# Experts with 96 slots a round in place of 128, in a two-layer decoder trunk

## The chip, the cores and the metric

The kernel runs on one core of one Trainium2 chip. The metric is the time of the execution on the device in microseconds (us), as the median of several runs; lower is better. The core's engines work side by side, each on its own list of instructions in order: TensorE (PE: matmuls, with its weight loads shown apart as PEld), VectorE (DVE), ScalarE (ACT), GpSimd (POOL) and SyncE (SP), whose queue issues nearly all DMA transfers.

## The reference

A trunk of two layers over 256 tokens of width 1024, in float32. Layer 0 is an RWKV-7 mixing followed by a dense SwiGLU, layer 1 a dilated attention followed by a mixture of 8 experts. The change touches the experts alone. In short:

```python
logits = ht @ router                        # 256 tokens x 8 experts
top_logit, top_idx = lax.top_k(logits, 2)   # two experts for each token
top_w = softmax(top_logit)
# for every expert e, over the tokens xe that chose it:
gt, up = split(xe @ w_gu[e])                # 1024 -> 2 x 3584
y = (silu(gt) * up) @ w_down[e]             # 3584 -> 1024
out[token] += y * weight of e for the token
```

The result goes through `x <- LayerNorm(sqrt(2)*x + (1+gate)*out)` and is the output. How many tokens choose an expert depends on the data; 256 is the most. The mean is 64.

## The kernel before

**The order of the work.** Up to the experts, an order written by a planner in the Python code holds: its class `Engine` (line 125) estimates what each instruction costs and when its inputs are due, and every task yields what it waits for. The routing task (`route_task`, line 2079) belongs to that part; it makes the first expert's slots and its dispatch. From `run_experts` (line 2184) on, instructions go to their engines in the order of the code, and a framework sets semaphores for each data dependency. Its scheduler may move an instruction that depends on little, such as the transfer of line 2244, ahead within its queue. Nearly every instruction is recorded through the helper on line 191, so the profile shows that line for most, and groups are told apart by the names of tiles.

**What an expert does.** Each token has, for each expert that it chose, a rank among that expert's tokens (`rank`, with large negative numbers for the others). `slots` compares the rank with the row `iota` 0, 1, 2, ... and gets a 0/1 matrix `P` of 2 x 128 tokens by 128 slots. `disp` multiplies the hidden states `hn` by `P`: the columns of `xh` and `xl` are the tokens in their slots, split into a float32r part and the rest. `slots_t` makes the transpose `PT` for the way back.

The weights come in pieces of 1 MB (`wstream`), and `split` makes `whi` (ScalarE) and `wlo` (VectorE) of each. `mm3` issues three matmuls for each weight tile: `xh*whi`, `xh*wlo`, `xl*whi`. The token operand (128 rows x 128 slots) is the stationary one, which a weight load brings into the array; 512 weight columns move. `gate` and `up` run over 8 tiles of 128 rows each for one of 7 stretches of 512 hidden columns; the product `e_s` is transposed by `tr` (four 128 x 128 transposes on TensorE, where `e_s` is stationary and the identity moves), split into `ah` (ScalarE) and `al` (VectorE), and `down` multiplies it by 4 tiles of 128 x 1024, accumulating in two PSUM banks. `fin` splits the sum into `yh` and `yl`, and `back` multiplies by `PT` and adds the weighted result to `macc`.

`run_experts` weaves these together: `tr` of the stretch before is issued inside `gate`, `down` of the stretch before comes between `gate` and `up`, and the slots and dispatch of the next expert (`part`) are issued inside `up` of stretch 4.

**What is left over.** An expert with more than 128 tokens has ranks of 128 and above, which match no slot. For these the code writes a table with ranks reduced by 128 to DRAM (lines 2237 to 2244), loads the highest count into a register (line 2245) and has an `If` around a loop over all 8 experts (line 2246):

```python
cv = nc.values_load(cmaxi[0:1, 0:1], min_val=0, max_val=512)
with tc.If(cv > 128):
    with tc.For_i(0, NE, 1) as ei:
```

After it comes the last LayerNorm, which begins with `bn_stats` on VectorE.

Of the kernel before, what the change touches and what calls it, by code (L numbers as in the profile page):

```python
# [24 lines left out]
F32 = mybir.dt.float32  # L25
F32R = mybir.dt.float32r
# [3 lines left out]
OP = mybir.AluOpType  # L30
AX = mybir.AxisListType

D = 1024
S = 256
DFF = 2816
NE = 8
# [5 lines left out]
RANK0 = 1000  # L42
NEG = -1.0e30
CW = 1029


def _consts():
# [44 lines left out]
def tile_kernel(ctx: ExitStack, tc: tile.TileContext, cst_d, att_d, x, c, ada_w, ada_b, ln_g, ln_b, mu, w_rkv,  # L92
# [3 lines left out]
    SY = nc.sync  # L96
# [97 lines left out]
    V, SC, GP, PE = Engine(nc.vector, "V"), Engine(nc.scalar, "SC"), Engine(nc.gpsimd, "GP"), Engine(nc.tensor, "PE")  # L194
# [9 lines left out]
    adap = ctx.enter_context(tc.tile_pool(name="adap", bufs=1, reuse_waits="tile"))  # L204
    kq = ctx.enter_context(tc.tile_pool(name="kq", bufs=1, reuse_waits="tile"))

    def mmt(j=None, shape=(128, 512)):
        if j is None:
            j = mm_n[0] = (mm_n[0] + 1) % 4
        return ringed(("mm", j), 1, mm_pool.tile(list(shape), F32, name="mmb", tag=f"mmb{j}"))  # L210
# [59 lines left out]
    ident, triS, iota = (cst[:, i:i + 128] for i in (0, 128, 256))  # L270
# [15 lines left out]
    ps = pst((128, 120))  # L286
# [7 lines left out]
    ps = pst((128, 112))  # L294
# [153 lines left out]
    def mm3(ps, lh, ll, rh, rl, start, stop):  # L448
        PE.matmul(ps, lh, rh, start=start, stop=False)
        PE.matmul(ps, lh, rl, start=False, stop=False)  # L450
        PE.matmul(ps, ll, rh, start=False, stop=stop)
# [209 lines left out]
    for t in range(2):  # L661
        for hf in range(2):
            ps = pst((128, 4, 128))
            for i in range(4):
                k = hf * 4 + i
# [812 lines left out]
    pn = ctx.enter_context(tc.tile_pool(name="pn", bufs=1, reuse_waits="tile"))  # L1478
# [31 lines left out]
    for j in range(6):  # L1510
        n = min(512, DFF - j * 512)
# [312 lines left out]
    hn, xtra, raw4 = [], [], []  # L1824
# [131 lines left out]
    e_n, ep, late = [0], [], {}  # L1956

    class Expert:
# [5 lines left out]

        def slots(self):

            self.P = ep[0].tile([128, 2, 128], F32, name="P", bufs=2)
            self.xh = ep[0].tile([128, 8, 128], F32R, name="xeh", bufs=2)
            self.xl = ep[0].tile([128, 8, 128], F32R, name="xel", bufs=2)
            for t in range(2):  # L1970
                V.tensor_scalar(self.P[:, t], iota, self.rcol(t), None, op0=OP.is_equal)

        def slots_t(self, ps):
            for t in range(2):
                PE.transpose(ps[:, t], self.P[:, t], ident)
            self.PT = ep[0].tile([128, 2, 128], F32R, name="PT", bufs=2)
            SC.copy(self.PT, ps)

        def disp(self, hf, ps):

            for i in range(4):
                k = hf * 4 + i
                for t in range(2):
                    PE.matmul(ps[:, i], hn[0][:, t, k * 128:(k + 1) * 128], self.P[:, t], start=t == 0, stop=t == 1)

        def disp_out(self, hf, ps):
            sl = slice(hf * 4, hf * 4 + 4)
            SC.copy(self.xh[:, sl], ps)
            V.tensor_tensor(self.xl[:, sl], ps, self.xh[:, sl].bitcast(F32), op=OP.subtract)

        def part(self, n):
            if n == 0:
# [6 lines left out]

        def half(self, c0, mid):  # L2000

            ps = mmt()
            for k, hi, lo in wstream(self.gu, D, c0, 512):
                mm3(ps, self.xh[:, k], self.xl[:, k], hi, lo, k == 0, k == 7)
                for f in mid.get(k, ()):
                    f()
            return ps

        def gate(self, j, mid):
            ps = self.half(j * 512, mid)  # L2010
            e_n[0] += 1
            self.s = pn.tile([128, 512], F32, name="e_s", tag=f"modtmp{e_n[0] % 2}")
            SC.activation(self.s, ps, AF.Silu)

        def up(self, j, mid):
# [4 lines left out]
        def tr(self):  # L2020
            ps = pst((128, 4, 128))
            for i in range(4):
                PE.transpose(ps[:, i], self.a[:, i * 128:(i + 1) * 128], ident)
            self.ah = ep[0].tile([128, 4, 128], F32R, name="ah", bufs=2)
            self.al = ep[0].tile([128, 4, 128], F32R, name="al", bufs=2)
            SC.copy(self.ah, ps)
            V.tensor_tensor(self.al, ps, self.ah.bitcast(F32), op=OP.subtract)

        def down(self, j, mid=(), fine=False):
            if j == 0:  # L2030
                self.y = [pt(0), pt(1)]
            ah, al = (self.ah, self.al)
            for k, hi, lo in wstream(self.dn[j * 512:(j + 1) * 512], 512, 0, D, fine):
                if k == 1:
                    for f in mid:
                        f()
                for hf in range(2):
                    csl = slice(hf * 512, (hf + 1) * 512)
                    mm3(self.y[hf], ah[:, k], al[:, k], hi[:, csl], lo[:, csl], j == 0 and k == 0,
                        j == 6 and k == 3)  # L2040

        def fin(self, last):
            self.yh = adap.tile([128, D], F32R, name="yh", tag="acc")
            self.yl = ep[0].tile([128, D], F32R, name="yl", tag="xel", bufs=2) if last else pn.tile(
                [128, D], F32R, name="yl", tag="lngb")
            for hf in range(2):
                csl = slice(hf * 512, (hf + 1) * 512)
                y = self.y[hf]
                if last:
                    y = pn.tile([128, 512], F32, name="e_s", tag=f"modtmp{hf}")  # L2050
                    V.tensor_tensor(y, self.y[hf], late["gate"][:, csl], op=OP.mult)
                SC.copy(self.yh[:, csl], y)
                V.tensor_tensor(self.yl[:, csl], y, self.yh[:, csl].bitcast(F32), op=OP.subtract)

        def back(self, t):
            for hf in range(2):
# [9 lines left out]
                else:  # L2066
# [10 lines left out]
                      lambda t, e=e: route["Wt"][:, t, e:e + 1], e == 0) for e in range(NE)]  # L2077
# [100 lines left out]
    Wt, rank, cmaxi = route["Wt"], route["rank"], route["cmaxi"]  # L2178
# [5 lines left out]
    def run_experts(exps, hook=None):  # L2184
        prev = old = None
        if exps[0].xh is None:
            for n in range(3):
                exps[0].part(n)
        for i, e in enumerate(exps):
            for j in range(7):  # L2190
                mg, mu_ = {}, {}
                if prev:
                    mg[1] = [prev[0].tr]
                if old and j == 1:
                    mg[5] = [lambda o=old: o.back(1)]
                nxt = exps[i + 1] if i + 1 < len(exps) else None
                if nxt and j == 4:
                    for n in range(3):
                        mu_.setdefault(1 + 3 * n, []).append(lambda e=nxt, n=n: e.part(n))
                e.gate(j, mg)  # L2200
                if not nxt and j == 6:
                    e.up(j, mu_)
                if prev:
                    prev[0].down(prev[1], [e.tr] if not nxt and j == 6 else ())
                    if prev[1] == 6:
                        old = prev[0]
                        old.fin(False)
                        mu_[5] = [lambda o=old: o.back(0)]
                if nxt or j < 6:
                    e.up(j, mu_)  # L2210
                prev = (e, j)
                if hook and i == len(exps) - 1 and j == 2:
                    hook()
        e.down(6, fine=True)
        e.fin(True)
        for t in range(2):
            e.back(t)
# [16 lines left out]
    run_experts(experts, moe_hook)  # L2234


    rank2 = ep[0].tile([128, 2, 8], F32, name="rank2")
    V.tensor_scalar(rank2, rank, -128.0, None, op0=OP.add)
    dtab = ctx.enter_context(tc.tile_pool(name="dtab", bufs=1, space=bass.MemoryType.DRAM))
    tab = dtab.tile([NE, 128, 4], F32, name="tab")  # L2240
    rw8 = ep[0].tile([128, NE, 4], F32, name="rw8")
    V.tensor_copy(rw8[:, :, 0:2], rank2.rearrange("p t e -> p e t"))
    V.tensor_copy(rw8[:, :, 2:4], Wt.rearrange("p t e -> p e t"))
    SY.dma_start(tab.rearrange("e p f -> p e f"), rw8)
    cv = nc.values_load(cmaxi[0:1, 0:1], min_val=0, max_val=512)
    with tc.If(cv > 128):
        with tc.For_i(0, NE, 1) as ei:
            rw1 = ep[0].tile([128, 4], F32, name="rw1")
            SY.dma_start(rw1, tab[bass.ds(ei, 1)].rearrange("e p f -> p (e f)"))
            run_experts([Expert(m_gu[0, bass.ds(ei, 1)].rearrange("e k n -> (e k) n"),  # L2250
                                m_dn[0, bass.ds(ei, 1)].rearrange("e k n -> (e k) n"),
                                lambda t: rw1[:, t:t + 1], lambda t: rw1[:, 2 + t:3 + t], False)])

    gb, bb = late["ln"]
    mvs = []
# [6 lines left out]
    for t in range(2):  # L2262
        for hf in range(2):
            csl = slice(hf * 512, (hf + 1) * 512)
            V.scalar_tensor_tensor(macc[t][:, csl], macc[t][:, csl], mvs[t][:, 0:1], gb[:, csl], op0=OP.subtract,
                                   op1=OP.mult)
    for t in range(2):
# [7 lines left out]
        for hf in range(2):  # L2275
            csl = slice(hf * 512, (hf + 1) * 512)
# [28 lines left out]
```

## Time and profile before

| | |
|---|---|
| Runs | 1826.45, 1823.01, 1826.03 us; median 1826.03 |
| Profiled execution | 1827.28 us |
| its span, first to last instruction | 1825.5 us |
| TensorE busy, share of the span | 1687.7 us, 92% |
| Weight loads | 1341.9 us, 74% |
| VectorE | 1499.5 us, 82% |
| ScalarE | 1136.4 us, 62% |
| GpSimd | 287.9 us, 16% |
| Moved by DMA | 498.95 MB, mean 273 GB/s |
| Mean granted TensorE clock | 0.962 of 2.4 GHz |

The span holds everything from the first to the last instruction; the profiled execution's own time has 1.8 us around it. A busy share is a mean over stages that have different limits. Matmuls overlap in the array, so a matmul's duration in the records is longer than its part of the time; the distance from one start to the next is what counts. A wait is put down to what released it last.

### The profile page before, as it was taken

Reading aid. Unit: us, or ns where it says so; the run is one execution under the profiler, and the core shown is the slowest. Engines: PE = TensorE matmul, PEld = TensorE weight load, DVE = VectorE, ACT = ScalarE, POOL = GpSimd, SP = SyncE. Lnnn points to the kernel's source line nnn. Section 1 sums busy time; section 2 is a strip of 40 time slices with the busy share of each in tenths; the row PEclk is TensorE's granted clock in tenths of the full one; section 3 lists DMA queues with packets and bytes.
Section 4 is the critical chain, followed back from the end, with each engine's and each line's share of the span. In section 5 each row is a group of like instructions: output and inputs, shape, how many; then the busy total and the mean of one; then the engine's idle time right before and its main releaser. Section 6 shows DMA issues by size and latency. Waiting matters only on the chain. (4 is left out here: it accounts for less than half of the span.)

```text
span 1825.5 us, 26566 instructions
## 1 busy us (share of the span) xinstructions
PE 1687.7 (92%) x9876; PEld 1341.9 (74%) x9876; DVE 1499.5 (82%) x2072; ACT 1136.4 (62%) x1542; POOL 287.9 (16%) x205
## 2 busy tenths in 40 slices
PE   6998888699997888879999999999999999999896
PEld 3686656478885666778888888888788787787784
DVE  2787786789967678579898898988988888988887
ACT  2445444255643656347777777877777777777673
POOL 0011111345414876320000000000000000000200
PEclk8999989799998999989999999999999999999998
DMA  9461551279884765478999999999999999999880
GB/s 333 146 188 62 182 188 36 81 284 334 306 296 143 241 231 177 143 286 303 332 358 374 353 350 355 367 355 338 347 346 359 347 352 348 348 350 342 308 319 25
DMA packets 213565, 498.95 MB, mean 273 GB/s; under 512 B 14634, under 2 KB 28818, under 8 KB 213428
## 3 DMA queue, kind: packets, MB, share of 16 engines
q1 hardware_dynamic: 212564, 494.03, 76.3%
q0 software_dynamic: 864, 3.15, 0.5%
q8 instruction: 79, 1.29, 0.3%
q14 instruction: 58, 0.48, 0.1%
HBM read 496.07 MB, written 1.06 MB: 272 GB/s over the span
## 5 line engine op out<-in xcount | busy, mean ns | idle before, releaser
L191 DVE TENSOR_TENSOR wlo<-raw,whi 128x1024 fp32r<-128x1024 f32 (+1 forms) x799 | 990.3, 1277 | 141.5 <-ACT whi L191 127.4
L191 ACT CAST whi<-raw 128x1024 fp32r<-128x1024 f32 x808 | 823.6, 1047 | 279.8 <-PE mmb L191 209.9
L191 PE MATMUL mmb<-wlo,xeh 128*128 128x512 f32 x896 | 356.6, 398 | 4.7 <-DVE wlo L191 4.0
L191 PE MATMUL mmb<-whi,xeh 128*128 128x512 f32 x896 | 353.4, 395 | 0.0
L191 PE MATMUL mmb<-whi,xel 128*128 128x512 f32 x896 | 352.1, 393 | 0.0
L191 PEld LDWEIGHTS mmb<-wlo,xeh 128*128 128x128 f32 x896 | 168.7, 188 | 46.7 <-DVE wlo L191 13.2
L191 PEld LDWEIGHTS mmb<-whi,xeh 128*128 128x128 f32 x896 | 168.8, 188 | 34.3 <-ACT whi L191 0.2
L191 PEld LDWEIGHTS mmb<-whi,xel 128*128 128x128 f32 x896 | 168.8, 188 | 32.7
L191 PE MATMUL psb<-wlo,ah 128*128 128x512 f32 x448 | 176.7, 394 | 1.5 <-DVE wlo L191 1.5
L191 PE MATMUL psb<-whi,al 128*128 128x512 f32 x448 | 174.9, 390 | 0.0
L191 PE MATMUL psb<-whi,ah 128*128 128x512 f32 x448 | 162.0, 392 | 0.0
L191 POOL TENSOR_TENSOR macc<-macc,gate 128x1024 f32<-128x1024 f32 x2 | 5.7, 2888 | 925.2 <-ACT gate L191 925.2
L191 POOL TENSOR_TENSOR acc<-acc,raw 128x512 f32<-128x512 f32 (+1 forms) x62 | 128.3, 2082 | 72.2 <-DVE acc L191 41.8
L191 PEld LDWEIGHTS psb<-wlo,ah 128*128 128x128 f32 x448 | 84.1, 188 | 24.7 <-DVE wlo L191 6.2
L191 PEld LDWEIGHTS psb<-whi,ah 128*128 128x128 f32 x448 | 83.5, 188 | 18.8 <-ACT whi L191 1.6
L191 PEld LDWEIGHTS psb<-whi,al 128*128 128x128 f32 x448 | 84.2, 188 | 16.4
L191 PE MATMUL mmb<-whi,f_xh 128*128 128x512 f32 (+1 forms) x192 | 74.1, 387 | 3.6 <-ACT f_xh L191 3.6
L191 PE MATMUL mmb<-whi,f_xl 128*128 128x512 f32 (+1 forms) x192 | 73.4, 382 | 1.9 <-DVE f_xl L191 1.9
L191 PE MATMUL mmb<-wlo,f_xh 128*128 128x512 f32 (+1 forms) x192 | 73.4, 382 | 0.2 <-DVE wlo L191 0.2
L191 ACT CAST ah<-psb 128x512 fp32r<-128x512 f32 x56 | 32.6, 583 | 61.0 <-PE psb L191 60.8
L191 ACT ACTIVATE e_s<-mmb 128x512 f32<-128x512 f32 x56 | 33.5, 599 | 44.9 <-PE mmb L191 44.9
L191 DVE TENSOR_TENSOR e_s<-e_s,mmb 128x512 f32<-128x512 f32 x56 | 38.3, 684 | 22.4 <-PE mmb L191 22.2
(429 smaller groups left out, 2559.8 us busy)
## 6 DMA issues: line engine op xcount, KB each, us to landing
raw<-in_moe_w_gu_dram SPq DMA_DIRECT2D x192, 1024.0 KB, 6.9
raw<-in_moe_w_down_dram SPq DMA_DIRECT2D x83, 1024.0 KB, 6.3
raw<-in_moe_w_gu_dram SPq DMA_DIRECT2D x60, 512.0 KB, 7.6
raw<-in_moe_w_down_dram SPq DMA_DIRECT2D x56, 512.0 KB, 6.0
raw<-in_ada_w_dram SPq DMA_DIRECT2D x37, 512.0 KB, 5.0
rawa<-in_ada_w_dram SPq DMA_DIRECT2D x35, 512.0 KB, 4.7
raw<-in_ada_w_dram SPq DMA_DIRECT2D x15, 1024.0 KB, 7.3
raw<-in_ffn_w_gu_dram SPq DMA_DIRECT2D x21, 512.0 KB, 5.6
```

The lines of the kernel that those rows point to most:

```text
L191: return fn(*a, **kw)
```

## The change

`CAP = 96` replaces 128 as the number of slots of a round, in the matrix `P`, the token operands, their transposes and the expert's intermediate tiles, which now lie on 96 of 128 partitions or have 96 columns. What is over runs in up to two more rounds (`ROUNDS` is 2), each with its table and its own `If` around a loop over all experts.

```diff
+CAP = 96
...
-            self.P = ep[0].tile([128, 2, 128], F32, name="P", bufs=2)
-            self.xh = ep[0].tile([128, 8, 128], F32R, name="xeh", bufs=2)
-            self.xl = ep[0].tile([128, 8, 128], F32R, name="xel", bufs=2)
+            self.P = ep[0].tile([128, 2, CAP], F32, name="P", bufs=2)
+            self.xh = ep[0].tile([128, 8, CAP], F32R, name="xeh", bufs=2)
+            self.xl = ep[0].tile([128, 8, CAP], F32R, name="xel", bufs=2)
...
-                PE.transpose(ps[:, t], self.P[:, t], ident)
-            self.PT = ep[0].tile([128, 2, 128], F32R, name="PT", bufs=2)
+                PE.transpose(ps[0:CAP, t], self.P[:, t], ident)
+            self.PT = ep[0].tile([CAP, 2, 128], F32R, name="PT", bufs=2)
...
-                    PE.matmul(ps[:, i], hn[0][:, t, k * 128:(k + 1) * 128], self.P[:, t], start=t == 0, stop=t == 1)
+                    PE.matmul(ps[:, i, 0:CAP], hn[0][:, t, k * 128:(k + 1) * 128], self.P[:, t], start=t == 0, stop=t == 1)
...
-            ps = mmt()
+            ps = mmt()[0:CAP]
             for k, hi, lo in wstream(self.gu, D, c0, 512):
                 mm3(ps, self.xh[:, k], self.xl[:, k], hi, lo, k == 0, k == 7)
...
-                PE.transpose(ps[:, i], self.a[:, i * 128:(i + 1) * 128], ident)
-            self.ah = ep[0].tile([128, 4, 128], F32R, name="ah", bufs=2)
-            self.al = ep[0].tile([128, 4, 128], F32R, name="al", bufs=2)
-            SC.copy(self.ah, ps)
-            V.tensor_tensor(self.al, ps, self.ah.bitcast(F32), op=OP.subtract)
+                PE.transpose(ps[:, i, 0:CAP], self.a[:, i * 128:(i + 1) * 128], ident[0:CAP, 0:CAP])
+            self.ah = ep[0].tile([128, 4, CAP], F32R, name="ah", bufs=2)
+            self.al = ep[0].tile([128, 4, CAP], F32R, name="al", bufs=2)
+            SC.copy(self.ah, ps[:, :, 0:CAP])
+            V.tensor_tensor(self.al, ps[:, :, 0:CAP], self.ah.bitcast(F32), op=OP.subtract)
...
-                    mm3(self.y[hf], ah[:, k], al[:, k], hi[:, csl], lo[:, csl], j == 0 and k == 0,
+                    mm3(self.y[hf][0:CAP], ah[:, k], al[:, k], hi[:, csl], lo[:, csl], j == 0 and k == 0,
...
-    rank2 = ep[0].tile([128, 2, 8], F32, name="rank2")
-    V.tensor_scalar(rank2, rank, -128.0, None, op0=OP.add)
...
-    with tc.If(cv > 128):
-        with tc.For_i(0, NE, 1) as ei:
...
+    ROUNDS = -(-S // CAP) - 1
+    tabs = []
+    rw8 = ep[0].tile([128, ROUNDS, NE, 4], F32, name="rw8")
+    for rd in range(ROUNDS):
+        V.tensor_scalar(rw8[:, rd, :, 0:2], rank.rearrange("p t e -> p e t"), -float(CAP * (rd + 1)), None, op0=OP.add)
+        V.tensor_copy(rw8[:, rd, :, 2:4], Wt.rearrange("p t e -> p e t"))
+        tabs.append(dtab.tile([NE, 128, 4], F32, name="tab", tag=f"tab{rd}"))
+        SY.dma_start(tabs[rd].rearrange("e p f -> p e f"), rw8[:, rd])
+    cv = nc.values_load(cmaxi[0:1, 0:1], min_val=0, max_val=512)
+    for rd in range(ROUNDS):
+        with tc.If(cv > CAP * (rd + 1)):
+            with tc.For_i(0, NE, 1) as ei:
...
```

`xl`, `yh`, `yl`, `e_s` and the reads of PSUM are cut to 96 in the same way. The weights, their pieces and their split stay as they are.

## Rows read from the trace of the kernel before

**Rows 1.** Busy time by engine in the experts' stretch, granted clock, DMA share.
```profile
core 0: us, PE busy (x) PEld busy (x) DVE busy (x) ACT busy (x) POOL busy (x), PEclk, DMA share, GB/s
801.40:1805.40 1004.00, 997.05 (x4569) 813.32 (x4566) 893.76 (x850) 752.98 (x819) 12.37 (x4) 1.00 0.93 334
```

**Rows 2.** Waits of SP's DMA queue, 801 to 1770 us: total, times, longest.
```profile
SPq L119 <- DVE wlo L191: 812.7, 369, 23.8
```

**Rows 3.** Waits of TensorE's weight loads in the experts' stretch.
```profile
PEld mmb L191 <- DVE wlo L191: 13.2, 28, 2.1
PEld psb L191 <- DVE wlo L191: 6.2, 13, 0.6
PEld psb L191 <- DVE e_s L191: 5.5, 18, 1.2
```

**Rows 4.** Groups of TensorE by form, experts: count | busy us, mean ns | idle.
```profile
L191 PE MATMUL mmb<-wlo,xeh 128*128 128x512 f32 x896 | 356.6, 398 | 4.7 <-DVE wlo L191 4.0
...
L191 PE MATMUL psb<-whi,ah 128*128 128x512 f32 x448 | 162.0, 392 | 0.0
L191 PE MATMUL psb<-cst,e_s 128*128 128x128 f32 x224 | 35.1, 279 | 0.8 <-DVE e_s L191 0.8
L191 PE MATMUL psb<-P,hn 128*128 128x128 f32 x228 | 31.2, 274 | 0.0
```

**Rows 5.** Timeline of TensorE from 1200 us: start, duration, instruction.
```profile
1199.98 0.39 PE L191 MATMUL mmb<-whi,xeh 128*128 128x512 f32 x1
...
1201.57 0.39 PE L191 MATMUL mmb<-wlo,xeh 128*128 128x512 f32 x1
```

**Rows 6.** Timeline of the router's weight loads, whose matmuls move 8 columns.
```profile
767.09 1.75 PEld L191 LDWEIGHTS mmb<-rt,modtmp 128*128 128x128 f32 x15
```

**Rows 7.** Timeline of TensorE, one transpose group, merged.
```profile
1795.17 0.60 PE L191 MATMUL psb<-cst,e_s 128*128 128x128 f32 x4
```

**Rows 8.** Timeline of two weight loads for transposes, early in the kernel.
```profile
18.82 0.20 PEld L191 LDWEIGHTS psb<-cst,row 128*128 128x128 f32 x2 [0.97 <-ACT row L191]
```

**Rows 9.** Timeline of TensorE after a stall in the experts.
```profile
1461.16 0.51 PE L191 MATMUL psb<-wlo,ah 128*128 128x512 f32 x1 [0.16 <-DVE wlo L191]
1461.51 0.40 PE L191 MATMUL psb<-whi,al 128*128 128x512 f32 x1
```

**Rows 10.** Weight loads: one group of the experts; those of cnt_w (min/median/max ns).
```profile
L191 PEld LDWEIGHTS mmb<-whi,xeh 128*128 128x128 f32 x896 | 168.8, 188 | 34.3 <-ACT whi L191 0.2
...
L191 PEld LDWEIGHTS <-cnt_w x5: 104/107/148, 794.0 to 794.6; 128*128 128x128 bf16 x5
```

**Rows 11.** Groups of VectorE and ScalarE by form in the experts' stretch.
```profile
L191 DVE TENSOR_TENSOR wlo<-raw,whi 128x1024 fp32r<-128x1024 f32 x668 | 792.3, 1229 | 69.1 <-ACT whi L191 55.4
L191 DVE TENSOR_TENSOR al<-psb,ah 128x512 fp32r<-128x512 f32 x56 | 38.4, 685 | 9.4 <-ACT ah L191 9.0
...
L191 ACT CAST whi<-raw 128x1024 fp32r<-128x1024 f32 x668 | 680.8, 1052 | 114.1 <-PE mmb L191 86.2 <-PE psb L191 24.3 <-issue 0.8
L191 ACT CAST ah<-psb 128x512 fp32r<-128x512 f32 x56 | 32.6, 583 | 61.0 <-PE psb L191 60.8
```

**Rows 12.** Instructions that write or read the tile rank.
```profile
L191 DVE TENSOR_SCALAR rank<-rank x1: 167/167/167, 796.5 to 796.5; 128x16 f32<-128x16 f32 x1
```

**Rows 13.** Instructions of the If (L2246), and VectorE's timeline behind it.
```profile
L2246 PEldq COMPARE_BRANCH  x1: 4072/4072/4072, 1808.2 to 1808.2; - x1
L2246 DVEq COMPARE_BRANCH  x1: 72/72/72, 1809.2 to 1809.2; - x1
...
L2246 DVEq EVENT_SEMAPHORE  x1: 21/21/21, 1812.1 to 1812.1; - x1
...
1812.23 1.88 DVE L191 BATCH_NORM_STATS2 bnst<-macc 128x6 f32<-128x512 f32 x3 [1.82 <-DVEq L2246]
```

**Rows 14.** Timeline of TensorE where the stationary's shape changes.
```profile
313.29 0.40 PE L191 MATMUL mmb<-whi,ygl 128*128 128x512 f32 x1
313.62 0.33 PE L191 MATMUL psb<-T,SM 64*64 64x64 f32 x4
```

More of the change, by code (lines that the diff above doesn't have):

```diff
@@ L1965, in slots @@
         def slots(self):
-            self.P = ep[0].tile([128, 2, 128], F32, name="P", bufs=2)
-            self.xh = ep[0].tile([128, 8, 128], F32R, name="xeh", bufs=2)
-            self.xl = ep[0].tile([128, 8, 128], F32R, name="xel", bufs=2)
+            self.P = ep[0].tile([128, 2, CAP], F32, name="P", bufs=2)
+            self.xh = ep[0].tile([128, 8, CAP], F32R, name="xeh", bufs=2)
+            self.xl = ep[0].tile([128, 8, CAP], F32R, name="xel", bufs=2)
             for t in range(2):
-                V.tensor_scalar(self.P[:, t], iota, self.rcol(t), None, op0=OP.is_equal)
+                V.tensor_scalar(self.P[:, t], iota[:, 0:CAP], self.rcol(t), None, op0=OP.is_equal)
         def slots_t(self, ps):
             for t in range(2):
-                PE.transpose(ps[:, t], self.P[:, t], ident)
-            self.PT = ep[0].tile([128, 2, 128], F32R, name="PT", bufs=2)
-            SC.copy(self.PT, ps)
+                PE.transpose(ps[0:CAP, t], self.P[:, t], ident)
+            self.PT = ep[0].tile([CAP, 2, 128], F32R, name="PT", bufs=2)
+            SC.copy(self.PT, ps[0:CAP])
         def disp(self, hf, ps):
@@ L1983, in disp @@
                 for t in range(2):
-                    PE.matmul(ps[:, i], hn[0][:, t, k * 128:(k + 1) * 128], self.P[:, t], start=t == 0, stop=t == 1)
+                    PE.matmul(ps[:, i, 0:CAP], hn[0][:, t, k * 128:(k + 1) * 128], self.P[:, t], start=t == 0, stop=t == 1)
         def disp_out(self, hf, ps):
             sl = slice(hf * 4, hf * 4 + 4)
-            SC.copy(self.xh[:, sl], ps)
-            V.tensor_tensor(self.xl[:, sl], ps, self.xh[:, sl].bitcast(F32), op=OP.subtract)
+            SC.copy(self.xh[:, sl], ps[:, :, 0:CAP])
+            V.tensor_tensor(self.xl[:, sl], ps[:, :, 0:CAP], self.xh[:, sl].bitcast(F32), op=OP.subtract)
         def part(self, n):
@@ L2011, in gate @@
             e_n[0] += 1
-            self.s = pn.tile([128, 512], F32, name="e_s", tag=f"modtmp{e_n[0] % 2}")
+            self.s = pn.tile([CAP, 512], F32, name="e_s", tag=f"modtmp{e_n[0] % 2}")
             SC.activation(self.s, ps, AF.Silu)
@@ L2038, in down @@
                     csl = slice(hf * 512, (hf + 1) * 512)
-                    mm3(self.y[hf], ah[:, k], al[:, k], hi[:, csl], lo[:, csl], j == 0 and k == 0,
+                    mm3(self.y[hf][0:CAP], ah[:, k], al[:, k], hi[:, csl], lo[:, csl], j == 0 and k == 0,
                         j == 6 and k == 3)
         def fin(self, last):
-            self.yh = adap.tile([128, D], F32R, name="yh", tag="acc")
-            self.yl = ep[0].tile([128, D], F32R, name="yl", tag="xel", bufs=2) if last else pn.tile(
-                [128, D], F32R, name="yl", tag="lngb")
+            self.yh = adap.tile([CAP, D], F32R, name="yh", tag="acc")
+            self.yl = ep[0].tile([CAP, D], F32R, name="yl", tag="xel", bufs=2) if last else pn.tile(
+                [CAP, D], F32R, name="yl", tag="lngb")
             for hf in range(2):
                 csl = slice(hf * 512, (hf + 1) * 512)
-                y = self.y[hf]
+                y = self.y[hf][0:CAP]
                 if last:
-                    y = pn.tile([128, 512], F32, name="e_s", tag=f"modtmp{hf}")
-                    V.tensor_tensor(y, self.y[hf], late["gate"][:, csl], op=OP.mult)
+                    y = pn.tile([CAP, 512], F32, name="e_s", tag=f"modtmp{hf}")
+                    V.tensor_tensor(y, self.y[hf][0:CAP], late["gate"][0:CAP, csl], op=OP.mult)
                 SC.copy(self.yh[:, csl], y)
@@ L2234, in tile_kernel @@
     run_experts(experts, moe_hook)
-    rank2 = ep[0].tile([128, 2, 8], F32, name="rank2")
-    V.tensor_scalar(rank2, rank, -128.0, None, op0=OP.add)
     dtab = ctx.enter_context(tc.tile_pool(name="dtab", bufs=1, space=bass.MemoryType.DRAM))
[L2240 to L2244, printed above, removed]
-    cv = nc.values_load(cmaxi[0:1, 0:1], min_val=0, max_val=512)
-    with tc.If(cv > 128):
-        with tc.For_i(0, NE, 1) as ei:
[L2248 to L2252, printed above, removed]
+    ROUNDS = -(-S // CAP) - 1
[6 more added lines that the diff above has]
+        SY.dma_start(tabs[rd].rearrange("e p f -> p e f"), rw8[:, rd])
+    cv = nc.values_load(cmaxi[0:1, 0:1], min_val=0, max_val=512)
+    for rd in range(ROUNDS):
+        with tc.If(cv > CAP * (rd + 1)):
+            with tc.For_i(0, NE, 1) as ei:
+                rw1 = ep[0].tile([128, 4], F32, name="rw1")
+                SY.dma_start(rw1, tabs[rd][bass.ds(ei, 1)].rearrange("e p f -> p (e f)"))
+                run_experts([Expert(m_gu[0, bass.ds(ei, 1)].rearrange("e k n -> (e k) n"),
+                                    m_dn[0, bass.ds(ei, 1)].rearrange("e k n -> (e k) n"),
+                                    lambda t: rw1[:, t:t + 1], lambda t: rw1[:, 2 + t:3 + t], False)])
     gb, bb = late["ln"]
```

## The prediction

> **What bounds the kernel now.** I read the windows first, to find the stage that the change touches: the experts run from 801.4 to 1805.4 us, 1004 of 1825.5 us of span, with TensorE busy for 997 of them, the granted clock at 1.00, that is 2.4 GHz, VectorE busy for 894 and ScalarE for 753 [rows 1]. The reader is to see that three resources look nearly full (TensorE, VectorE, and the DMA engines at a share of 0.93), so the page's shares alone do not say which of them sets the pace. The waits do. The queue that loads weights spends 812.7 us waiting for VectorE to hand back a raw buffer [rows 2], so transfers run ahead and are not the bound. TensorE's weight loads wait 24.9 us for VectorE (13.2 + 6.2 + 5.5, 59 times) [rows 3]. So TensorE is the bound, with some 25 us of stalls from VectorE that a lighter VectorE could give back.
>
> Next the groups of instructions, to see what TensorE is busy with. The six groups of expert matmuls (three of 896 and three of 448, first and last shown) hold 4032 instructions, beside 224 transposes of the hidden tile and 228 dispatch records [rows 4]. A mean of 398 ns is no price, because matmuls overlap; the price is the distance from start to start. Of eight that stand in a row, the first starts at 1199.98 and the last at 1201.57: 1.59 us over 7 distances, 227 ns [rows 5]. 4032 x 0.227 = 915 us: nine tenths of the stage is this one form.
>
> **The change part by part.**
>
> *The 4032 expert matmuls.* 96 slots make the stationary operand 96 columns wide instead of 128; the moving operand stays 512 weight columns. 512 columns at 2.4 GHz are 213 ns, so moving columns account for nearly all of the 227, and their number does not change. The weight load gets shorter, but it lies beside the matmul before it: a load of 128 columns takes 0.11 us of the array's time when nothing hides it (15 loads with 8 moving columns in 1.75 us, less 0.19 for one, over 14) [rows 6], against 0.227 of cover. I take 0. The bound below is that the 13-14 ns above the 213 shrink with the columns: a quarter of them, 3.3 ns x 4032 = 13.4 us. Above, the nearest row is the cost of changing the array's shape, a rival below.
>
> *The 224 transposes in tr.* Here the 96 columns are on the moving side (the identity is cut to 96 x 96). Four of them take 0.60 us; less 0.28 for the last, over 3, that is 0.107 each [rows 4, 7]. Is that moving time or load time? Two loads for a transpose lie within 0.20 us, 0.06 apart, where the matmuls don't hold them [rows 8]; so the load needs 0.06 and the 0.107 is moving time. Three quarters of it is 0.080: 0.027 x 224 = 6.0 us less. Bounds: 0, if another limit holds it at 0.107, and 6.0.
>
> *The 228 dispatch records (disp).* P moves with 96 columns, but the stationary is still 128 columns of hn, in plain float32, and records of this kind with only 8 moving columns stand 0.11 us apart [rows 6]. They are bound by their load. I take 0; the other bound is 0.027 x 228 = 6.2 us less.
>
> *Loads that a stall uncovers.* After a wait, the matmul starts at 1461.16 and the next at 1461.51: 0.35 instead of 0.23, the 0.11-0.12 being the load that had no cover [rows 9]. Of the 59 waits, 41 are for a weight tile and are followed by such a load of xe or ah; a quarter of 0.11 is 0.027, x 41 = 1.1 us less (bounds 0 and, for all 59, 1.6).
>
> A rule of the Trainium skill speaks against this part. What the row shows: a load of xeh takes 188 ns, one of cnt_w, 128 columns of bf16, 107 [rows 10]. The skill's page "TensorE: Matmul & The Clock Gate", section "Weight-path perf modes — Fast Weight Load (FWL) and DoubleRow", says that a quick weight load is on only for a full 128 columns and not for FP32, so that 96 columns would lose it. If fp32r had it at 128, each of the 41 uncovered loads would become 81 ns longer, +3.3 us in place of -1.1. The 188 says that fp32r does not have it, so nothing is lost.
>
> *VectorE and ScalarE.* al and xel (72 instructions) and ah and xeh shrink from 512 to 384 elements a partition. VectorE takes 1229 ns for 1024 and 685 for 512, 1.06 a column, so 136 ns less each, 9.8 us in all; ScalarE (1052 - 583)/512 = 0.92, 117 ns less each, 8.4 us [rows 11]. What runs on 96 instead of 128 partitions (Silu, the product, yh, yl) keeps its length, since that goes by the columns. None of it is on the path but through the 59 stalls. A stall behind ah and al can shorten by both, 0.25 us, x 59 = 14.9; but TensorE comes 0.11 us earlier per tr, which eats nearly half of it, and most stalls stand behind weight tiles further on. I take 2 us (bounds 0 and 14.9).
>
> *The tables.* One more small VectorE instruction of 167 ns, where the routing leads into the experts [rows 12], +0.2 us, and one more table transfer on SP at about 846 us, among loads that run ahead. Bounds 0 and 0.2; if loads were late, the transfer would be seen.
>
> *The second If.* Every engine now passes two skipped bodies. VectorE's branch starts at 1809.2 and its next instruction at 1812.1, 2.9 us later, although its last macc was done at 1810.4: bnst starts at 1812.23 after 1.82 us of idleness put down to that line [rows 13]. Nothing hides it: bnst opens the final LayerNorm, the end of the kernel. The first branch keeps its place behind the experts, the second can only be reached when the first has landed, so +2.9 us on the end. Bounds: 0.07, if only the compare is paid, and 4.07, what TensorE's branch took. SP, ScalarE, POOL and TensorE pay too, but have nothing left to do or wait for VectorE.
>
> Sum: -6.0 - 1.1 - 2.0 + 0.2 + 2.9 = -6.0 us. The profiled execution took 1827.28 us, so 1821.3; it stands 1.25 above the median of the three runs (1826.03), so 1820 for a median. The bounds add up to -42 and +4 without a change of shape.
>
> **Rivals.**
>
> *No gain, the branch stays.* The transposes stay at 0.107, the stalls move instead of shrinking, and +3.1 is left: 1829. For it: VectorE is busy for 89% of the stage, so time won on TensorE may return as waiting. Against: VectorE's load falls by 9.8 us, more than TensorE's. This is within what can be told from no change.
>
> *The array's shape.* If 96 columns count as another shape than 128, TensorE drains at every change. Where it goes from a 512-column matmul with a 128-column stationary to 64 x 64 ones, the next starts 0.33 us later and not 0.23 [rows 14], 0.10 more. Stationaries of 128 columns (transposes, dispatch, back) stand between those of 96: 2 x 56 around tr, 4 x 7 around disp, 4 x 8 around back, 172 changes, 17.2 us: 1837, slower. It decides from 97 changes on (slower by over 3.65 us needs 9.7). Against it: nothing before uses 96 columns, so no row shows it at all. The Trainium skill's page "TensorEngine Tiling (Array Packing)", section "Tiling Modes", has shapes of 128, 64 and 32 columns alone and says that changing the mode drains the array; by it, 96 run as 128 and there is no change. That the 0.10 is such a drain, the trace agrees.
>
> *The fixed part shrinks with the columns*, 13.4 us more: 1807. For it, 13-14 ns that moving columns do not explain; against, no row connects them with the load.
>
> *VectorE was the real limit*, and the stalls give back their 14.9: 1807. For it, the 59 waits name VectorE; against, TensorE is busy for 997 of 1004.
>
> *The fast load is lost*: 4.4 us from the forecast, 1824. The load rows speak against it.
>
> *The extra round runs*, if an expert has over 96 tokens. Counting the reference's choices for its default input gives 63, 74, 79, 77, 55, 49, 54 and 61, so it does not; other draws reach 97 to 102. A round repeats the whole stage: 1820 + 1004 = 2824.
>
> **How the numbers follow.** A measurement here tells some 0.2%, 3.65 us, from no change. Chances: the forecast 0.43 (its own bounds 1816 to 1824), no gain 0.20, change of shape 0.11, fixed part 0.10, VectorE 0.08, fast load lost 0.03, extra round 0.02, and 0.03 for work that another order makes late. Faster: 0.40 of the forecast, 0.10 and 0.08, 0.58. Same: no gain, the fast load and a little of the forecast, 0.25. Slower: 0.11, 0.02, 0.03 and a sliver of "no gain", 0.17. The range runs from 1806, which takes in the two rivals at 1807, to 1832, which takes in "no gain"; a change of shape and the extra round stay out.
>
> **What would show it.** Right: expert matmuls still 227 ns apart, transposes about 80, dispatch records still 110, al near 549 and ah near 466 ns, two branches on VectorE about 3 us each in the tail, the stage some 9 us shorter. Wrong: matmuls at 224, a distance of 0.33 around tr, waits on VectorE gone or grown by over 5 us, or body instructions between the branches.

## The result, and the profile after

The changed kernel takes 1841.48 us (median of 1841.49, 1844.42, 1841.47 and 1839.44), the kernel before 1826.03: a ratio of 1.0076, with a 95% interval from 1.0062 to 1.0091. It is slower by some 14 us (15.5 between the medians, 13.9 by the ratio), where 6 us less were forecast, and outside the stated range. The profiled execution is one of the four, 1841.49 us with a span of 1839.7, 14.2 more than the span before.

The experts' stretch (same view as [rows 1]) has grown by 9.3 us, from 1004.0 to 1013.3, although TensorE's weight loads, VectorE and ScalarE are all less busy; the granted clock is 1.00 as before:

```profile
802.40:1815.70 1013.30, 1002.93 (x4568) 703.07 (x4566) 886.90 (x850) 743.38 (x819) 12.37 (x4) 1.00 0.92 331
```

The groups of TensorE and of its loads, as in [rows 4] and [rows 10] (count | busy us, mean ns | idle). A load of xeh takes 162 ns and not 188:

```profile
L192 PE MATMUL mmb<-wlo,xeh 128*96 128x512 f32 x896 | 356.3, 398 | 7.6 <-DVE wlo L192 7.1
...
L192 PE MATMUL psb<-whi,ah 128*96 128x512 f32 x448 | 161.4, 393 | 0.0
L192 PE MATMUL psb<-P,hn 128*128 128x96 f32 x228 | 29.6, 271 | 0.0
L192 PE MATMUL psb<-cst,e_s 96*128 96x96 f32 x224 | 27.9, 246 | 0.8 <-DVE e_s L192 0.8
...
L192 PEld LDWEIGHTS mmb<-wlo,xeh 128*96 128x96 f32 x896 | 144.8, 162 | 77.7 <-DVE wlo L192 21.4
```

These means hide the loss: 398 ns stands in both kernels. It shows in the distances. The timeline gives the first and the last of 24 expert matmuls in a row (start us, duration, instruction):

```profile
913.77 0.39 PE L192 MATMUL mmb<-whi,xeh 128*96 128x512 f32 x1
...
919.09 0.40 PE L192 MATMUL mmb<-whi,xel 128*96 128x512 f32 x1
```

5.32 us over 23 distances are 231 ns, where [rows 5] gave 227. Over the whole stage, the distances below 260 ns from an expert matmul to the next matmul of 512 columns have a mean of 227.97 ns before (3755 of them) and 231.47 after (3774). With the stalls behind them, the 4032 take 943.9 us before and 957.3 after, by the sums of their distances to the next matmul of any kind: +13.4. The transposes (as [rows 7]) take less, 0.50 us for four in place of 0.60; over all 224, 16.1 us in place of 20.9:

```profile
1028.77 0.50 PE L192 MATMUL psb<-cst,e_s 96*128 96x96 f32 x4
```

In the tail, the two skipped bodies (as [rows 13]) keep VectorE idle for 6.02 us ahead of bnst and not 1.82:

```profile
L2249 PEldq COMPARE_BRANCH  x2: 3608/4264/4921, 1818.4 to 1822.3; - x2
...
L2249 DVEq COMPARE_BRANCH  x2: 56/64/72, 1819.4 to 1822.8; - x2
...
L2249 DVEq EVENT_SEMAPHORE  x2: 21/21/21, 1822.7 to 1826.6; - x2
...
1826.68 0.69 DVE L192 BATCH_NORM_STATS2 bnst<-macc 128x6 f32<-128x512 f32 x1 [6.02 <-DVEq L2249]
```

So the 14.2 us are: matmuls +13.4, transposes -4.9, dispatch and the way back +0.8 (the stage: +9.3), the tail +4.0 (20.5 to 24.5 us from the start of the last expert matmul), and a stage that begins 1.0 us later. The last is no finding: over the runs of this study the stage begins between 797 and 806 us.

### The profile page after: what moved, and what is told of

Read it like the earlier page. It is cut to its first block, busy times and chain, and to the rows that moved or that the text cites. A ratio compares the mean times of both kernels' runs of the same rounds, so it can differ in the third digit from the quotient of the medians.

```text
span 1839.7 us, 26576 instructions
## 1 busy us (share of the span) xinstructions
PE 1693.8 (92%) x9875; PEld 1232.1 (67%) x9875; DVE 1490.8 (81%) x2073; ACT 1126.2 (61%) x1542; POOL 288.1 (16%) x205
## 5 line engine op out<-in xcount | busy, mean ns | idle before, releaser
L192 PE MATMUL mmb<-wlo,xeh 128*96 128x512 f32 x896 | 356.3, 398 | 7.6 <-DVE wlo L192 7.1
L192 PE MATMUL mmb<-whi,xel 128*96 128x512 f32 x896 | 354.5, 396 | 0.0
L192 PE MATMUL mmb<-whi,xeh 128*96 128x512 f32 x896 | 354.4, 396 | 0.0
L192 PEld LDWEIGHTS mmb<-wlo,xeh 128*96 128x96 f32 x896 | 144.8, 162 | 77.7 <-DVE wlo L192 21.4
L192 PEld LDWEIGHTS mmb<-whi,xeh 128*96 128x96 f32 x896 | 144.6, 161 | 58.4
L192 PEld LDWEIGHTS mmb<-whi,xel 128*96 128x96 f32 x896 | 144.8, 162 | 55.7
L192 PE MATMUL psb<-wlo,ah 128*96 128x512 f32 x448 | 177.5, 396 | 2.0 <-DVE wlo L192 0.7
L192 PE MATMUL psb<-whi,al 128*96 128x512 f32 x448 | 176.1, 393 | 0.0
L192 PE MATMUL psb<-whi,ah 128*96 128x512 f32 x448 | 161.4, 393 | 0.0
L192 PEld LDWEIGHTS psb<-wlo,ah 128*96 128x96 f32 x448 | 72.3, 161 | 38.7 <-DVE wlo L192 8.4
```

The costliest lines, as they stand in the source:

```text
L192: return fn(*a, **kw)
```

## The experiments

The question was why a matmul whose moving operand is unchanged takes 3.5 ns longer. First theories: C, the 96 columns themselves; L, the layout, because the rows of a narrow tile begin every 384 bytes and not every 512. "Distance" below is the mean over the run of the distances under 260 ns from an expert matmul to the next matmul of 512 columns; "stage" is the time from the first expert matmul's start to the last one's end, 1004.0 us before.

**e1: 96 columns in rows of 512 bytes.**

```diff
-self.xh = ep[0].tile([128, 8, CAP], F32R, name="xeh", bufs=2)
+self.xh = ep[0].tile([128, 8, 128], F32R, name="xeh", bufs=2)[:, :, 0:CAP]
...  # xl, ah and al likewise
```

> Changed kernel with xeh, xel, ah and al laid out 128 wide as before, of which 96 columns are used: only their place and stride in memory differ from the changed kernel. Theory C (a stationary operand of 96 columns itself makes each 512-column matmul dearer): the distance from start to start stays at a mean of 231 to 232 ns among the 4032 expert matmuls, the time near 1841 us. Theory L (the 384-byte rows of the narrow tiles are read less well, by the weight load or beside it): the distance goes back to 228 ns, the time falls by about 13 us to 1828.

Measured: distance 230.19, ratio to before 1.0067 (1.0049 to 1.0085). The timeline has 5.29 us over 23:

```profile
1018.14 0.39 PE L192 MATMUL mmb<-whi,xeh 128*96 128x512 f32 x1
...
1023.43 0.39 PE L192 MATMUL mmb<-whi,xel 128*96 128x512 f32 x1
```

Neither theory alone: a third of the loss goes, two thirds stay. But the distances have become even. In the changed kernel those that begin with a wlo matmul go 228.6, 232.7, 229.2, 230.7, 229.5, 232.5, 229.2, 232.3 over the 8 tiles of xeh, whose rows start 384 bytes apart; in e1 they lie between 229.8 and 230.6. Where a tile's row begins does matter.

**e2: 128 columns read, rows of 384 bytes.**

```diff
+c = slice(k * CAP, k * CAP + 128)
-mm3(ps, self.xh[:, k], self.xl[:, k], hi, lo, k == 0, k == 7)
+mm3(ps, self.xhf[:, c], self.xlf[:, c], hi, lo, k == 0, k == 7)
...  # tiles flat, with 32 filled columns at the end; ah and al likewise
```

> Changed kernel whose expert matmuls read 128 stationary columns out of the 96-wide tiles (the last 32 of a read are the next tile's first columns, and 32 filled ones at the end); rows 96 to 127 of the sums are thrown away. Layout as in the changed kernel, column count as before. Theory C: distance back to 228 ns, stage about 13 us shorter, time near 1828 us. Theory L: distance stays at 231 to 232 ns, time near 1841 us. Both: the tail keeps the two branches.

Measured: distance 231.82, ratio 1.0108 (1.0088 to 1.0127). 5.33 us over 23, with all 128 columns:

```profile
952.47 0.39 PE L192 MATMUL mmb<-whi,xeh 128*128 128x512 f32 x1
...
957.80 0.39 PE L192 MATMUL mmb<-whi,xel 128*128 128x512 f32 x1
```

C falls as the whole explanation: with full columns the loss is there, 3.8 ns a matmul.

**e3: 112 slots**, `CAP = 112`.

> 112 slots in place of 96, all else as changed (still two further rounds). Theory C with a step (anything short of 128 costs the same): distance 231 to 232 ns. Theory C in proportion to the missing columns: about 229.8 ns, time near 1835 us. Theory L (rows of 448 bytes): either, but then e1 says 228. Transposes near 0.094 us apart in each case.

Measured: distance 231.58, ratio 1.0081 (1.0057 to 1.0105). No proportion to the missing columns; but rows of 448 bytes change the layout as well, and only e6 below separates the two. Transposes at 0.082 from start to start, as a mean over their groups, between 0.072 at 96 and 0.094 at 128.

**e4: the kernel before with a second If** of the same body behind the first.

```diff
+with tc.If(cv > 192):
+    with tc.For_i(0, NE, 1) as ei:
...
```

> The kernel before with a second If and loop of the same body behind the first, never entered: the tail's part of the change alone. If the second skipped body costs what the changed kernel's trace shows: VectorE idle before the last bnst 5.5 to 6.5 us in place of 1.8, experts' stage unchanged at 1004 us, time 1829 to 1831 us. Rival (the tail's loss came from other waits on the narrower tiles): idle stays at 1.8 us, 1826 us.

Measured: ratio 1.0023 (1.0013 to 1.0032), 4 us; distance 227.93, stage 1004.0; VectorE's idle time ahead of bnst 5.7 us. The tail's part is the second skipped body, and it has nothing to do with the stage.

After these, theory S held that a matmul needs full columns and rows of 512 bytes; its rival E, that something else in the narrow expert disturbs TensorE.

**e5: e1 with 128 columns read** (the last 32 filled by GpSimd), and the second If inside the first.

```diff
+for f_ in (self.ahf, self.alf):
+    GP.tensor_copy(f_[:, :, CAP:], ones.rearrange("p (a b) -> p a b", b=32))
...  # xeh and xel likewise
-mm3(self.y[hf][0:CAP], ah[:, k], al[:, k], hi[:, csl], lo[:, csl], j == 0 and k == 0,
+mm3(self.y[hf], ah[:, k], al[:, k], hi[:, csl], lo[:, csl], j == 0 and k == 0,
```

> Changed kernel with xeh, xel, ah and al 128 wide, the last 32 columns filled by GpSimd, and expert matmuls that read all 128; the second If stands inside the first, so that one skipped body is left. Transposes, evictions and slots stay at 96. Theory S (a matmul costs its 227 to 228 ns only where the stationary's 128 columns are full and each starts at a multiple of 512 bytes from the tile's start; e1 and e2 each broke one of the two): distance back to 227 to 228 ns, transposes 0.07 to 0.08, experts' stage 998 to 1001 us, VectorE idle before bnst 1.8 us, time 1821 to 1824, some 4 us under the kernel before. Theory E (something else of the narrow expert, its 96 partitions or lighter evictions, disturbs TensorE): distance stays at 230 to 232, stage near 1011, time 1834 to 1838.

Measured: distance 228.02, 5.21 us over 23; ratio 1.0008 (0.9997 to 1.0018), stage 1006.1.

```profile
907.24 0.39 PE L192 MATMUL mmb<-whi,xeh 128*128 128x512 f32 x1
...
912.45 0.39 PE L192 MATMUL mmb<-whi,xel 128*128 128x512 f32 x1
```

E falls: the expert is as narrow as in the changed kernel everywhere else, and the matmuls are back. S passes on the distance. But the stage did not fall to 1000, nor the time to 1824: the transposes gave 4.3 us, and the gaps (the distances above 260 ns, counted by what each has above 228) grew from 26.0 us to 31.3.

**e6: e1 with 112 slots.**

> e1 with 112 slots in place of 96: rows of 512 bytes, 112 columns read. Theory S, any count short of 128: an even distance near 230 ns for every one of the 8 tiles. Theory S in proportion: near 229. Theory E: as e1 or between.

Measured: distance 230.75, 1842.44 us in one run. Fewer than 128 columns in rows of 512 bytes cost 2 to 3 ns, 96 no more than 112.

**e7: the kernel before, the experts' tiles 32 bytes further.**

```diff
+ep[0].tile([128, 8], F32, name="gap")
 xtra.extend(ep[0].tile([128, 1024], F32, name="raw", tag=tag, bufs=2) for tag in ("xeh", "xel"))
```

> Kernel before with a gap of 32 bytes ahead of the experts' tiles, so that xeh, xel, ah and al start at a multiple of 256 bytes and not 32 bytes short of one; 128 columns, 512-byte rows. If the start of a row counts in fine steps: distance differs from 227.97 by over 0.5 ns (a higher one: up to 232, time up to 1842; a lower one: the later half of the stage, now 228.4, falls to 227.3, time 2 to 4 us less). If only the distance between rows counts: 228 and 1828.

Measured: distance 233.18, ratio 1.0076 (1.0060 to 1.0091). A gap of 32 bytes alone, with no instruction changed, costs as much as the whole change:

```profile
916.70 0.40 PE L191 MATMUL mmb<-whi,xeh 128*128 128x512 f32 x1
...
922.06 0.40 PE L191 MATMUL mmb<-whi,xel 128*128 128x512 f32 x1
```

S was too narrow: full columns in rows of 512 bytes are not enough.

**e8: the changed kernel with the second If inside the first.**

```diff
+with tc.If(cv > CAP):
+    round_(0)
+    with tc.If(cv > 2 * CAP):
+        round_(1)
```

> Changed kernel with the second If inside the first one's body, nothing else. One skipped body in the tail: VectorE idle before bnst back to 1.8 us, tail from the last expert matmul 20.3 us in place of 24.3, expert matmuls as in the changed kernel (231 to 232 ns), time near 1837 us. Rival (the skip costs by the length of the body skipped, which is now double): idle 4 to 6 us, time 1841.

Measured: ratio 1.0054 (1.0037 to 1.0070), against 1.0076 with two; distance 231.45. VectorE's idle time is back at 1.88 us, although the one body that is skipped is now twice as long:

```profile
1821.93 0.69 DVE L192 BATCH_NORM_STATS2 bnst<-macc 128x6 f32<-128x512 f32 x1 [1.88 <-DVEq L2256]
```

**e9: the kernel before, all tiles 32 bytes further.**

```diff
+cp.tile([128, 8], F32, name="gap")
 cst = cp.tile([128, 384], F32, name="cst")
```

> Kernel before with 32 unused bytes at the very start of the on-chip memory, so that every later tile, stationary, moving weights, raw pieces and all, moves by 32 bytes; in e7 only the experts' stationary tiles moved. If the place in itself decides: expert matmuls 233 ns apart as in e7, and the dense layer's matmuls (f_xh, 227.7 in every run so far) slow down as well, time 1843 or more. If the place of the stationary against the moving weights decides: 228 ns and 227.7, time 1828.

Measured: distance 227.96, dense layer 227.6 as before, ratio 1.0000 (0.9990 to 1.0011). 5.21 us over 23:

```profile
964.19 0.39 PE L191 MATMUL mmb<-whi,xeh 128*128 128x512 f32 x1
...
969.40 0.39 PE L191 MATMUL mmb<-whi,xel 128*128 128x512 f32 x1
```

xeh lies at the very address that it has in e7, since both gaps are 32 bytes and lie ahead of it. There the weights stayed behind and the distance was 233; here they moved along and it is 228. So the place itself does not decide. What counts is the place of the stationary rows against what stayed behind in e7, and of that these matmuls read only the moving weights.

**e10: e5 with two lasting pairs of ah and al**, each filled once.

```diff
+apair.append([ep[0].tile([128, 4, 128], F32R, name=n_, bufs=2) for n_ in ("ah", "al")])
...
+self.ahf, self.alf = apair[(e_n[1] - 1) % 2]
```

> e5 with two lasting pairs of ah and al, whose last 32 columns GpSimd fills once and not for every stretch. e5's matmuls were back at 228.0 ns and its transposes at 0.0745, but stalls grew from 26 to 31 us. If the fills made these stalls: stage 998 to 1001, time 1823 to 1826 beside 1828.9 of before. If the time won on TensorE comes back as waiting for VectorE: stage 1003 to 1006, time 1828 to 1830.

Measured: ratio 1.0021 (1.0009 to 1.0033), distance 227.96, stage 1005.2, gaps 30.9 us. Its waits against [rows 3], total, times, longest:

```profile
PEld mmb L192 <- DVE wlo L192: 17.1, 29, 2.1
PEld psb L192 <- DVE wlo L192: 8.7, 17, 0.7
PEld psb L192 <- DVE e_s L192: 4.9, 16, 1.2
```

30.7 us in place of 24.9. The fills were not the reason. Transposes 4.5 us shorter, waiting 5.8 longer: what TensorE won came back as waiting for VectorE, as its second expectation had it. Why VectorE, with 7.6 us less in al, is no earlier was not settled.

**e11 and e12: e10 with 64 and with 128 bytes ahead of the experts' tiles.**

```diff
+ep[0].tile([128, 16], F32, name="gap")   # e12: [128, 32]
```

> e10 with a gap of 64 bytes ahead of the experts' tiles. If the place counts by 64 bytes (half of a row's place in 64 stays): distance 228 as in e10. If it counts by a longer stretch: 229 to 234.

> e10 with a gap of 128 bytes ahead of the experts' tiles. If the place counts by 64 or 128 bytes: 228 as in e10. If by 256 or more: 229 to 234, and e11 likewise.

Measured: 233.30 and 232.51, at 1848.27 and 1847.11 us, one run each; over 23 distances 5.37 us in e11 and 5.34 in e12:

```profile
898.33 0.40 PE L192 MATMUL mmb<-whi,xeh 128*128 128x512 f32 x1
...
903.70 0.39 PE L192 MATMUL mmb<-whi,xel 128*128 128x512 f32 x1
```

```profile
1152.79 0.40 PE L192 MATMUL mmb<-whi,xeh 128*128 128x512 f32 x1
...
1158.13 0.39 PE L192 MATMUL mmb<-whi,xel 128*128 128x512 f32 x1
```

All three shifts that were tried (32, 64, 128 bytes) are bad. In the good layouts, the rows of xeh and of whi lie a multiple of 256 bytes apart, by the addresses that the program gives its tiles; in the kernel before, the distances with weights at a multiple of 512 from the stationary have a mean of 228.1 ns, and those with weights 256 off 227.8. This is not the whole rule: in e2, 230.2 ns lie between matmuls whose own stationary and the next one are both at a multiple of 256.

No version was faster than the kernel before: e5 and e9 are level with it.

## Why the prediction was wrong

**The step that failed** is the first: "The 4032 expert matmuls", costed at 0, with a bound above that came only from a change of the array's shape. The argument was that the moving columns stay at 512 and the shorter load is covered. Both hold, and the load did get shorter, 188 to 162 ns. What was left out is that the 13 to 14 ns beyond the 213 of the moving columns are no constant: they go up by as much as 5.2 ns with the place of the stationary's rows against the moving ones (e7 against e9) and by 2.2 with 96 columns at a good place (e1 against e5). The changed kernel has both: 384-byte rows, whose starts come to lie 128 bytes off for every other tile, and short columns. In place of 0 the term measured 3.5 ns x 3774 distances = 13.2 us. The two causes do not add up: 384-byte rows alone cost 3.8 ns (e2), short columns alone 2.2, both together 3.5; why is open. I had seen this fixed part and made a rival of it, but only with a sign that helps, "a quarter of them, 3.3 ns x 4032 = 13.4 us" less. That this has the size of the measured loss is chance: it was a quarter of the fixed part, and the place of the rows did not come into it.

**The other steps.** The transposes: 0.107 to 0.080 forecast, -6.0 us; measured -4.9 over their distances. The mechanism (moving columns) was right. In the changed kernel these 4.9 us count in full in the sum above; in e5 and e10, with the matmuls back at 228, they came back as waiting and the stage was no shorter. The dispatch records: forecast 0, measured +0.5 (22.0 to 22.5 us), which fits records that are bound by their load. The tables' 0.2 us cannot be told: they would show in the start of the stage, which differs by 8 us between runs. Evictions: al 551 ns (forecast 549), ah 476 (466):

```profile
L192 DVE TENSOR_TENSOR al<-psb,ah 128x384 fp32r<-128x384 f32 x56 | 30.8, 551 | 7.7 <-ACT ah L192 7.4
...
L192 ACT CAST ah<-psb 128x384 fp32r<-128x384 f32 x56 | 26.7, 476 | 68.6 <-PE psb L192 68.4
```

What was to follow from them, 3.1 us less of stalls and uncovered loads, did not: the waits of [rows 3] grew from 24.9 to 34.1 us,

```profile
PEld mmb L192 <- DVE wlo L192: 21.4, 49, 2.2
PEld psb L192 <- DVE wlo L192: 8.4, 15, 0.8
PEld psb L192 <- DVE e_s L192: 4.3, 16, 1.2
```

a growth of 9.2 us, more than the 5 that the prediction had named as a sign of being wrong. The gaps between the matmuls stayed all the same (26.0 and 25.9 us). That shorter loads can begin later and still be in time would explain both; it is argued, not shown.

The second If: 2.9 forecast, 4.2 measured on VectorE's idle time (the two branches took 3.3 and 3.8 us, the one of before 2.9), 4.0 on the tail. Mechanism right, as e4 and e8 show; term a third too small, because the two branches took longer than the one of before from which it was read. Why they differ is open.

**The rivals.** The change of shape came nearest in time (1837) and is refuted in its mechanism: 24 matmuls with no change of shape between them are already 5 ns apiece slower (5.32 us over 23 distances, against 5.21 in e9), and e2 has the loss with 128-column stationaries. The quick weight load: the Trainium skill's page "TensorE: Matmul & The Clock Gate", section "LDWEIGHTS (loading the stationary operand)", has a load go by its columns at 1.2 GHz. That makes, as an estimate, 27 ns less for 32 fewer; the trace agrees on the difference, with 26, and not on the length: 188 ns for 128 columns, where the page's rule would give some 107. So nothing was lost on the load itself. "VectorE was the real limit" fails: VectorE was busy 7 us less, and the gaps gave nothing back. The extra round did not run: the stage has 4568 matmul records, against 4569 before. "No gain, the branch stays" was right that the stalls do not shrink and, without the slower matmuls, too small.

## What to carry to other kernels

When a tile is made narrower, its rows and often the tiles behind it move in the memory: look at where stationary rows lie against the moving ones before counting columns, and test a suspected layout with a dead gap of a few bytes, once ahead of one operand and once ahead of both. A price that is the distance between two starts has a fixed part; ask for its bound in both directions, however constant it looks in one layout. A skipped body at the end of a kernel costs its branch in full, so rounds that rarely run belong inside one another.

## What the runs showed of the hardware that was not expected

- Two float32r matmuls of 512 moving columns follow each other after 228.0 ns, as the mean of the stage, where the stationary rows lie well against the moving ones (e9 and e10; 226.7 in the 24 of e9 above), and after 233.2 and 233.3 with the stationary 32 or 64 bytes off (e7, e11), 232.5 with 128 (e12), at the same granted clock of 1.00 and with the same instructions. What in the reading makes this difference, no run shows.
- A stationary with 96 of 128 columns, at the good place, costs 2.2 ns more a matmul (230.19, e1, against 228.02, e5), and 112 columns cost 2.7 (230.75, e6, one run): less to load, longer to the next matmul. Why is not shown.
- Before, the distance is 227.3 ns up to 1200 us and 228.4 from then on; e4, e5, e9 and e10 have the same rise, the layouts that are off do not. This stays open.
